# Reciprocal square roots by a GpSimd power throughout, and query projections filled up to 128 rows

## The chip, the cores and the metric

The kernel runs on one core of a Trainium2 chip. The metric is device time in microseconds (us) of one execution, from the first to the last instruction and what lies around it. The five engines are TensorE (PE in the profile, with its weight loads PEld), VectorE (DVE), ScalarE (ACT), GpSimd (POOL) and SyncE (SP, which issues the DMAs).

## The reference

Two transformer blocks follow one another on 512 tokens of 1024 features; the second also carries 256 context tokens. Everything is float32.

```python
def first_block(...):                      # once
    h = rmsnorm(x) * (1 + sc1) + sh1       # sc, sh, g: c_act @ w_ada
    q_a, k_a, v_a, q_d, k_d, v_d, z_d, b_d, a_d = split(h @ w_in)
    y_attn  = dilated_attention(q_a, k_a, v_a, rel_bias)      # 8 heads
    q, k, v = split(silu(causal_conv(concat(q_d, k_d, v_d))))
    q, k    = l2norm(q) * 64 ** -0.5, l2norm(k)               # per head
    o       = chunk_gated_delta_rule(q, k, v, g(a_d), sigmoid(b_d))
    y_delta = rmsnorm(o, norm_g) * silu(z_d)                  # per head
    x = x + g1 * (concat(y_attn, y_delta) @ w_out)
    x = x + g2 * swiglu(rmsnorm(x) ...)
def second_block(...):                     # two layers
    # half step of a gated FFN on h and on the context
    z  = modulate(rms_norm(h)) @ w_in      # 1376 columns
    q  = rms_norm(z[..., 256:448], g_q) @ w_uq       # 192 -> 4 heads x 96
    kv = rms_norm(z[..., 448:576], g_kv) @ w_ukv     # 128 -> 4 heads x 128
    # Fourier mixer, attention over h and context, gating unit
    # (its v is rms-normed per head), pooling mixer; then w_out
    # second half step; the context goes on only in layer 0
```

Every rmsnorm and l2norm takes one reciprocal square root per token, or per token and head.

## The kernel before, in words

Activations lie as 128 features by tokens. A weight comes in units of 128x1024: SP loads it (L183), ScalarE rounds it to a form that TensorE reads in one pass ("whi", L186), VectorE makes the rest ("wlo", L187), and a product takes three passes: whi by the high part of the activation, whi by its low part, wlo by its high part (`mm`, L128). Products of plain float32 operands are issued as one instruction each and take two passes in the trace. Transposes and broadcasts along features also go through TensorE (`tr`, L162).

The code is written as generators that a planner of the kernel interleaves. It counts the columns of every matmul (`mm` adds them to `self.clock`), and a generator's `yield 2.0` says after how many us of such work it wants to go on. The order of the instructions on each engine comes from the tile framework's scheduler, which weighs what each instruction costs and what it waits for; so a change of instructions on VectorE can move rows of the other engines too.

Reciprocal square roots come from one helper, `rsqrt` (L87). Up to two columns it is a scaling on VectorE (L97) and a power of -0.5 on GpSimd (L98). From three columns on it is eleven small VectorE instructions (L108 to L118): the scaling, a first guess from the bits, and two rounds of correction. Sixteen places have more than two columns: the first norm "n1" (128x4, L1470); in each of the four pairs of heads of the delta net one for q and k (128x16, `delta`, L728, tiles rsxd to rsyd) and one for the output (128x8, L895); in the second block the key and query norms of the latent tokens (128x4, `col_rsqrt`, L984, two in each layer) and the gating unit (128x16 twice, 128x8 once, L1283). All other norms have two columns.

In the first block, `delta_prep` (L667) makes the convolutions of q, k and v of a pair of heads (tiles "cv", L682), `delta_gates` (L614) makes decay and beta (gu, gs, gpoly, gx, then a matmul psg and gc), and `delta` (L688) goes on: GpSimd multiplies the decay matrices by masks (L717, L719), TensorE sums squares of q and k into psT, `rsqrt` follows, VectorE copies its result to rq (L730), ScalarE spreads it (L660), and TensorE transposes that to psb (L162), on which the rest of the pair stands. Attention tiles of other heads and weight products fill TensorE between.

In the second block `kvq` (L992) makes queries. The 192 normed features lie in two tiles, c0 (128 rows) and c1 (64 rows), and the weights in `wuq[0]` (128 rows) and `wuq[1]` (64 rows, `small_w`, L953). `pq(j)` (L1073) multiplies 128 columns of weights in two matmuls, the second of 64 rows:

```python
self.mm(ps[:, :T], self.wuq[0][:, j*P : (j+1)*P], c0[:, :T], True, False)
self.mm(ps[:, :T], self.wuq[1][0:64, j*P : (j+1)*P], c1[0:64, :T], False, True)
```

There are eleven such products: four for the latent tokens (T = 512) in each layer and three for the context (T = 256) in layer 0.

Of the kernel before, what the change touches and what calls it, by code (L numbers as in the profile page):

```python
# [9 lines left out]
F32 = mybir.dt.float32  # L10
F32R = mybir.dt.float32r
BF16 = mybir.dt.bfloat16
I32 = mybir.dt.int32
U8 = mybir.dt.uint8
AF = mybir.ActivationFunctionType
ALU = mybir.AluOpType
# [13 lines left out]
P = 128  # L30
# [3 lines left out]
EPS = 1e-6  # L34
# [47 lines left out]
class Kernel:  # L82
# [4 lines left out]
    def rsqrt(self, v, scale, shape, key):  # L87

        nc, sm = self.nc, self.small
        n = 1  # L90
        for d in shape[1:]:
            n *= d
        if n <= 2:
            x = sm.tile([P, n], F32, tag="rs_x", name=f"rsx{key}")
            y = sm.tile([P, n], F32, tag="rs_y", name=f"rsy{key}")
            xv = x.rearrange("p (a b) -> p a b", a=shape[1]) if len(shape) == 3 else x
            nc.vector.tensor_scalar(xv, v, float(scale), EPS, op0=ALU.mult, op1=ALU.add)  # L97
            nc.gpsimd.tensor_tensor(out=y, in0=x, in1=self.minus_half[:, 0:n], op=ALU.pow)  # L98
            return y
        x = sm.tile([P, n], F32, tag="rs_x", name=f"rsx{key}")  # L100
        y = sm.tile([P, n], F32, tag="rs_y", name=f"rsy{key}")
        a = sm.tile([P, n], F32, tag="rs_a", name=f"rsa{key}")
        b = sm.tile([P, n], F32, tag="rs_b", name=f"rsb{key}")
        xv = x
        if len(shape) == 3:
            xv = x.rearrange("p (a b) -> p a b", a=shape[1])
        V = nc.vector
        V.tensor_scalar(xv, v, float(scale), EPS, op0=ALU.mult, op1=ALU.add)  # L108
        V.tensor_scalar(y.bitcast(I32), x.bitcast(I32), -0.5, float(0x5F1FFFF9), op0=ALU.mult, op1=ALU.add)
        V.tensor_mul(a, y, y)  # L110
        V.tensor_mul(a, a, x)
        V.tensor_scalar(a, a, -0.703952253, 0.703952253 * 2.38924456, op0=ALU.mult, op1=ALU.add)
        V.tensor_mul(y, y, a)
        V.tensor_mul(a, y, y)
        V.tensor_mul(a, a, x)
        V.scalar_tensor_tensor(b, a, -10.0 / 3.0, a, op0=ALU.add, op1=ALU.mult)
        V.tensor_scalar(b, b, 0.375, 1.875, op0=ALU.mult, op1=ALU.add)
        V.tensor_mul(y, y, b)  # L118
        return y

    def ax1(self, name):
# [831 lines left out]
    def small_w(self, l, keep):  # L953

        nc, A, G = self.nc, self.A, self.G
        self.gcols = self.cp.tile([P, 8], F32, tag=f"gcols{l}", name=f"gcols{l}")
        nc.sync.dma_start(out=self.gcols, in_=A["gcols"][l])
        self.wukv = G.get("k" if keep else "t", "k")
        nc.sync.dma_start(out=self.wukv, in_=A["w_ukv"][l])
        self.wuq = [G.get("k" if keep else "t", "k"), G.get("k" if keep else "t", "k")]  # L960
        nc.sync.dma_start(out=self.wuq[0], in_=A["w_uq"][l, 0:128])
        nc.sync.dma_start(out=self.wuq[1][0:64, :], in_=A["w_uq"][l, 128:192])

    def zproj(self, s, u):


        halves = s.T == TL and any(x[2][0] is s for x in self.later)
        w = self.wunit(self.W2, u)
        ps = self.mm1("pz")
        for c0, c1 in ((0, 256), (256, 512)) if halves else ((0, s.T),):  # L970
            self.settle(s, c0, c1)
            for k in range(KD):
                ah, al = (x[:, c0:c1] for x in s.h[k][:2])
                wh, wl = w[0][:, k * P : (k + 1) * P], w[1][:, k * P : (k + 1) * P]
                self.mm(ps[:, c0:c1], wh, ah, k == 0, False)
                self.mm(ps[:, c0:c1], wh, al, False, False)
                self.mm(ps[:, c0:c1], wl, ah, False, k == KD - 1)
                if k == 3 or (c1 - c0 == TL and k in (1, 5)):
                    yield 1.3
            if c1 < s.T:  # L980
                yield 1.3
        return ps
# [9 lines left out]
    def kvq(self, s, l, rope, key, query):  # L992

        nc, V, G = self.nc, self.nc.vector, self.G
        T = s.T
        kh, vv = s.kv(l)
        s.vv = vv
        ps = yield from self.zproj(s, 0)
        held = []

        def pair():
            if T == TL:
                return G.get("t", "k"), G.get("t", "k")
            x = G.get("t", "k")
            held.append(x)
            return x[:, 0:T], x[:, T : 2 * T]
# [8 lines left out]
        ps = yield from self.zproj(s, 1)  # L1015
        if query:
            c1, sq1 = pair()
            nc.scalar.activation(sq1[0:64, :T], ps[0:64, :T], AF.Square)
            nc.scalar.activation(c1[0:64, :T], ps[0:64, :T], AF.Identity, scale=self.gcols[0:64, 2:3])
        if rope is not None:  # L1020
# [13 lines left out]
        if query:  # L1034
            ps = yield from self.zproj(s, 2)
# [13 lines left out]
        for j in range(2):  # L1049
            ps = self.ax1("pk")  # L1050
# [8 lines left out]
        for t in range(0, s.ntt, 2):  # L1059
            ps = self.ax1("pv")  # L1060
# [12 lines left out]
        def pq(j):  # L1073
            ps = self.ax1("pqh")
            self.mm(ps[:, :T], self.wuq[0][:, j * P : (j + 1) * P], c0[:, :T], True, False)
            self.mm(ps[:, :T], self.wuq[1][0:64, j * P : (j + 1) * P], c1[0:64, :T], False, True)
            return ps
        pr = pq(2)
        if rope is not None:
            t1, t2 = G.get("t", "k"), G.get("t", "k")  # L1080
            V.tensor_mul(t1, pr, rope[0])
            yield 1.7
            pr = pq(3)
            V.tensor_mul(t2, pr, rope[1])
            V.tensor_add(t1, t1, t2)
            yield 1.7
            for h in range(4):
                (nc.scalar.copy if h % 2 else V.tensor_copy)(qh[h][64:96, :], t1[32 * h : 32 * h + 32, :])
            G.put(t1, t2)
        else:  # L1090
            for h in range(4):
                (nc.scalar.copy if h % 2 else V.tensor_copy)(qh[h][64:96, :T], pr[32 * h : 32 * h + 32, :T])
            yield 0.9
        for j in range(2):
            ps = pq(j)
            for a in range(2):
                (nc.scalar.copy if a else V.tensor_copy)(qh[2 * j + a][0:64, :T], ps[64 * a : 64 * a + 64, :T])
            yield 1.7 * T / TL
# [320 lines left out]
    def build_(self, st, stop):  # L1419
        tc, nc, A = self.tc, self.nc, self.A  # L1420
# [21 lines left out]
        G = self.G  # L1442
        self.ones = self.cp.tile([P, 2], F32, tag="ones", name="ones")
        nc.vector.memset(self.ones, 1.0)
        self.minus_half = self.cp.tile([P, 8], F32, tag="mhalf", name="mhalf")
        nc.vector.memset(self.minus_half, -0.5)
        cv = self.load_cvec("cva", A["c"])
        mods = self.cp.tile([P, 48], F32, tag="mods1", name="mods1")
# [36 lines left out]
        for k in range(KD):  # L1485
# [9 lines left out]
            n = len(first)  # L1495
# [34 lines left out]
        v = []  # L1530
# [21 lines left out]
        for t in range(4):  # L1552
            f = collections.deque([attn] * MUL[t][0])
# [463 lines left out]
```

## Time and profile before

| what | us |
|---|---|
| time, median of 3 runs (lowest to highest) | 3309.32 (3308.56 to 3309.61) |
| profiled execution | 3308.47 |
| its span, first to last instruction | 3306.7 |
| PE busy | 3241.5 (98%) |
| DVE busy | 2036.8 (62%) |
| ACT busy | 1065.2 (32%) |
| POOL busy | 58.5 (2%) |

The span lies 1.8 us below the execution's own time. Busy time is counted from start to end of an instruction. In the timeline a row gives start, duration, engine, line, operation with out<-in, the number of instructions taken together, and in brackets the idle time of the engine ahead of it and what ended it. A 512-column pass follows the one before in some 0.21 to 0.23 us though the row of a single one reads 0.39, because the row runs from start to modelled end.

### The profile page before, as it was taken

The page shows a single profiled execution, that of the slowest core. Times are in us where ns is not written, and L with a number is a line of the kernel's source. Part 1 is how long each engine was busy: PE and PEld are TensorE (multiplying, and loading weights), DVE is VectorE, ACT ScalarE, POOL GpSimd, SP SyncE. Part 2 cuts the span into 40 slices and gives each one's busy share as a digit, 9 for nine tenths or more (in the row PEclk, how much of TensorE's full clock was granted, in tenths as well). Part 3 has the DMA queues.
Part 4 walks back from the last instruction along what each step waited for, and adds up shares of the span by engine and source line. Part 5 has one row for each costly group of instructions (what it writes and reads, how often), then busy time and mean ns, then how long its engine had stood idle before and what let it go on. Part 6 is the DMA issues. An engine that isn't in the chain of part 4 may idle for free.

```text
span 3306.7 us, 45936 instructions
## 1 busy us (share of the span) xinstructions
PE 3241.5 (98%) x18536; PEld 2705.1 (82%) x18536; DVE 2036.8 (62%) x3812; ACT 1065.2 (32%) x1782; POOL 58.5 (2%) x95
## 2 busy tenths in 40 slices
PE   6999999999999999999999999999999999999998
PEld 5778788888888888977888888888888888798887
DVE  7777785776856556667865454585554447673334
ACT  4444342224222222436522222242221235542222
POOL 0101000000000000000000000000000000000000
PEclk9999999999999999999999999999999999999999
DMA  8333254542433333222133232233332212233331
GB/s 268 103 111 95 81 158 153 161 145 78 159 97 106 103 107 100 83 87 90 58 120 96 83 101 85 88 101 110 112 106 83 89 52 79 60 109 96 96 96 58
DMA packets 105321, 344.12 MB, mean 104 GB/s; under 512 B 14402, under 2 KB 20459, under 8 KB 105108
## 3 DMA queue, kind: packets, MB, share of 16 engines
q1 hardware_dynamic: 105108, 341.17, 33.1%
q8 instruction: 146, 2.39, 0.3%
q14 instruction: 67, 0.55, 0.0%
HBM read 339.01 MB, written 4.74 MB: 104 GB/s over the span
## 4 chain that ended last, share of the span: by engine, by line
PE 93%; DVE 4%; issue 1%; ACT 1%; DMA 1%; POOL 0%; SPq 0%; POOLq 0%; DVEq 0%; ACTq 0%
PE psg L128 24%; PE psu L128 24%; PE psd L128 21%; PE psdc L128 6%; PE pz L128 4%; PE pp L128 3%; PE pss L128 2%; PE pso L128 2%; PE psv L128 2%; PE psY L128 1%; PE pst L162 1%; PE pqh L128 1%; DVE dump L246 0%; DVE wlo_w_in L187 0%; PE psb L162 0%
## 5 line engine op out<-in xcount | busy, mean ns | idle before, releaser
L186 ACT CAST whi_f<-wraw_f 128x1024 fp32r<-128x1024 f32 x264 | 276.5, 1050 | 716.6 <-PE psdc L128 238.1
L187 DVE TENSOR_TENSOR wlo_f<-wraw_f,whi_f 128x1024 fp32r<-128x1024 f32 x264 | 322.6, 1223 | 205.9 <-ACT whi_f L186 199.7
L128 PE MATMUL psu<-r,whi_f 128*128 128x512 f32 (+1 forms) x1504 | 446.1, 379 | 0.0
L128 PE MATMUL psg<-r,whi_f 128*128 128x512 f32 (+1 forms) x1504 | 443.8, 377 | 0.0
L128 PEld LDWEIGHTS psu<-r,whi_f 128*128 128x128 f32 x1504 | 277.1, 189 | 55.8
L128 PE MATMUL psd<-r,whi_f 128*128 128x512 f32 (+1 forms) x1152 | 321.8, 358 | 0.2 <-DVE xl L497 0.2
L128 PEld LDWEIGHTS psg<-r,whi_f 128*128 128x128 f32 x1504 | 273.2, 188 | 51.9
L408 DVE TENSOR_TENSOR sg<-sg,psu 128x512 f32<-128x512 f32 x110 | 75.5, 686 | 383.6 <-PE psu L128 382.3
L246 DVE CUSTOM_DVE_ANT_0 dump<-ada_w_ada,cva 128x1024 bf16<-128x1024 f32 x192 | 234.6, 1222 | 119.7 <-DMA ada_w_ada<-in_w_ada 118.8
L128 PE MATMUL psu<-r,wlo_f 128*128 128x512 f32 (+1 forms) x752 | 285.1, 379 | 0.0
L128 PE MATMUL psg<-r,wlo_f 128*128 128x512 f32 (+1 forms) x752 | 284.1, 378 | 0.0
L497 DVE SCALAR_TENSOR_TENSOR xl<-psd,ml,xl 128x512 f32<-128x512 f32 (+1 forms) x272 | 176.4, 654 | 152.4 <-PE psd L128 151.1
L128 PEld LDWEIGHTS psd<-r,whi_f 128*128 128x128 f32 x1152 | 184.4, 188 | 20.9 <-DVE xl L497 0.5
L128 PE MATMUL psu<-c,whi_f 128*128 128x512 f32 x528 | 189.5, 397 | 0.0
L128 PE MATMUL psg<-c,whi_f 128*128 128x512 f32 x528 | 188.3, 395 | 0.0
L128 PE MATMUL psd<-r,wlo_f 128*128 128x512 f32 (+1 forms) x528 | 187.3, 355 | 0.0
L128 PEld LDWEIGHTS psu<-r,wlo_f 128*128 128x128 f32 x752 | 141.8, 189 | 28.1
L128 PEld LDWEIGHTS psg<-r,wlo_f 128*128 128x128 f32 x752 | 141.6, 188 | 26.9
L497 DVE SCALAR_TENSOR_TENSOR xc<-psdc,mc,xc 128x256 f32<-128x256 f32 x320 | 150.6, 478 | 6.5 <-PE psdc L128 4.2
L128 PE MATMUL psdc<-r,whi_f 128*128 128x512 f32 x392 | 151.9, 393 | 0.0
L128 PE MATMUL psd<-y,whi_f 128*128 128x512 f32 (+1 forms) x512 | 150.9, 362 | 0.0
L128 PE MATMUL psu<-c,wlo_f 128*128 128x256 f32 x528 | 149.0, 282 | 0.0
(758 smaller groups left out, 6328.0 us busy)
## 6 DMA issues: line engine op xcount, KB each, us to landing
wraw_f<-in_f SPq DMA_DIRECT2D x264, 512.0 KB, 3.5
ada_w_ada<-in_w_ada SPq DMA_DIRECT2D x192, 512.0 KB, 3.6
wraw_ffn<-in_ffn SPq DMA_DIRECT2D x66, 512.0 KB, 3.6
wraw_w_in<-in_w_in SPq DMA_DIRECT2D x64, 512.0 KB, 3.5
wraw_w_out<-in_w_out SPq DMA_DIRECT2D x28, 512.0 KB, 3.5
bias<-bias SPq DMA_DIRECT2D x8, 320.0 KB, 5.7
xl<-in_x SPq DMA_DIRECT2D x8, 256.0 KB, 7.7
k<-bias SPq DMA_DIRECT2D x8, 256.0 KB, 3.6
```

What stands on the lines that cost most here:

```text
L128: self.nc.tensor.matmul(out, lhsT=lhsT, rhs=rhs, start=start, stop=stop)
L162: self.nc.tensor.transpose(out, in_, self.ident[:k, :k])
L186: nc.scalar.copy(hi, raw)
L187: nc.vector.tensor_sub(lo, raw, hi.bitcast(F32))
L246: job = nc.vector.tensor_tensor_reduce(out=dump, in0=raw, in1=cv, scale=1.0, scalar=0.0, op0=ALU.mult, op1=ALU.add, accum_out=dst[:, nb : ...
L408: nc.vector.tensor_mul(sg, sg, pu)
L497: nc.vector.scalar_tensor_tensor(x, q, gates[s][:, m : m + 1], x, op0=ALU.mult, op1=ALU.add)
```

## The change

Two edits. `rsqrt` loses its eleven-instruction form: all sixteen places above now do what the two-column places did, one VectorE scaling (now L96) and one GpSimd power (now L97); the tile of exponents grows from 8 to 16 columns. And the second tile of the query weights and of the normed query features get zeros in rows 64 to 127, written by GpSimd, so that both matmuls of `pq` read 128 rows.

```diff
@@ rsqrt
-        if n <= 2:
-            ...
-            return y
         x = sm.tile([P, n], F32, tag="rs_x", name=f"rsx{key}")
         y = sm.tile([P, n], F32, tag="rs_y", name=f"rsy{key}")
-        a = sm.tile([P, n], F32, tag="rs_a", name=f"rsa{key}")
-        b = sm.tile([P, n], F32, tag="rs_b", name=f"rsb{key}")
-        ...
-        V.tensor_scalar(xv, v, float(scale), EPS, op0=ALU.mult, op1=ALU.add)
-        V.tensor_scalar(y.bitcast(I32), x.bitcast(I32), -0.5, float(0x5F1FFFF9), op0=ALU.mult, op1=ALU.add)
-        V.tensor_mul(a, y, y)
-        V.tensor_mul(a, a, x)
-        ...
-        V.tensor_mul(y, y, b)
+        xv = x.rearrange("p (a b) -> p a b", a=shape[1]) if len(shape) == 3 else x
+        nc.vector.tensor_scalar(xv, v, float(scale), EPS, op0=ALU.mult, op1=ALU.add)
+        nc.gpsimd.tensor_tensor(out=y, in0=x, in1=self.minus_half[:, 0:n], op=ALU.pow)
         return y
@@ small_w
         nc.sync.dma_start(out=self.wuq[1][0:64, :], in_=A["w_uq"][l, 128:192])
+        nc.gpsimd.memset(self.wuq[1][64:128, :], 0.0)
@@ kvq
             c1, sq1 = pair()
+            nc.gpsimd.memset(c1[64:128, :T], 0.0)
@@ pq
-            self.mm(ps[:, :T], self.wuq[1][0:64, j * P : (j + 1) * P], c1[0:64, :T], False, True)
+            self.mm(ps[:, :T], self.wuq[1][:, j * P : (j + 1) * P], c1[:, :T], False, True)
@@ build
-        self.minus_half = self.cp.tile([P, 8], F32, tag="mhalf", name="mhalf")
+        self.minus_half = self.cp.tile([P, 16], F32, tag="mhalf", name="mhalf")
```

Line numbers after the helper fall by 21. On PE the order of the rows changes in the first block alone; from there on it stays. Three places show it.

On POOL at the first pair of heads, before: a copy and a clearing, then the six multiplications by masks (k is a slot of an arena, m_low and m_cum are masks), then clearings of tiles for the next step.

```order
L774 COPY k_19_141<-id_487 128x512
L801 MEMSET k_21_143 64x512
L717 ISA
L717 TENSOR_TENSOR k_6_128<-k_7_129,m_low 64x4x64 x2
L719 TENSOR_TENSOR k_7_129<-k_7_129,m_cum 128x512
L717 TENSOR_TENSOR k_6_128<-k_0_122,m_low 64x4x64 x2
L719 TENSOR_TENSOR k_0_122<-k_0_122,m_cum 128x512
L849 MEMSET k_16_138 128x512
L850 MEMSET k_17_139 128x512
```

On POOL at the same place, after:

```order
L753 COPY k_19_141<-id_476 128x512
L780 MEMSET k_21_143 64x512
L696 TENSOR_TENSOR k_6_128<-k_7_129,m_low 64x4x64 x2
L696 TENSOR_TENSOR k_6_128<-k_0_122,m_low 64x4x64
L698 TENSOR_TENSOR k_7_129<-k_7_129,m_cum 128x512
L696 TENSOR_TENSOR k_6_128<-k_0_122,m_low 64x4x64
L698 TENSOR_TENSOR k_0_122<-k_0_122,m_cum 128x512
L97 TENSOR_TENSOR rsyd_681<-rsxd_680,mhalf 128x16
L828 MEMSET k_16_138 128x512
```

A power (rsyd from rsxd, 16 columns) has come in behind the six multiplications and ahead of the clearings, and one multiplication by m_low now stands ahead of the first by m_cum.

On DVE at the first convolutions, before: wlo_w_in_8 is the low part of the eighth weight unit, cv a convolution step; gx, beta and gs belong to the gates.

```order
L187 TENSOR_TENSOR wlo_w_in_8_565<-wraw_w_in_8_562,whi_w_in_8_564 128x1024
L682 SCALAR_TENSOR_TENSOR cv<-pp,conv_w,cv 128x511
L631 TENSOR_TENSOR gx<-psT,dtb 128x32
L682 SCALAR_TENSOR_TENSOR cv<-pp,conv_w,cv 128x510
L633 TENSOR_SCALAR beta<-beta 128x32
L645 TENSOR_SCALAR gx<-gx 128x32
L682 SCALAR_TENSOR_TENSOR cv<-pp,conv_w,cv 128x509
L634 RECIPROCAL beta<-beta 128x32
L637 TENSOR_SCALAR gs<-gu 128x32
L682 SCALAR_TENSOR_TENSOR cv<-pp,conv_w,cv 128x511
L638 RECIPROCAL gs<-gs 128x32
```

On DVE around the same weight unit, after:

```order
L661 SCALAR_TENSOR_TENSOR cv<-pp,conv_w,cv 128x511
L613 RECIPROCAL beta<-beta 128x32
L616 TENSOR_SCALAR gs<-gu 128x32
L661 SCALAR_TENSOR_TENSOR cv<-pp,conv_w,cv 128x510
L617 RECIPROCAL gs<-gs 128x32
L661 SCALAR_TENSOR_TENSOR cv<-pp,conv_w,cv 128x509
L618 TENSOR_TENSOR gs<-gs,gu 128x32
L166 TENSOR_TENSOR wlo_w_in_8_554<-wraw_w_in_8_551,whi_w_in_8_553 128x1024
L619 TENSOR_TENSOR gs_495<-gs 128x32
L661 SCALAR_TENSOR_TENSOR cv<-pp,conv_w,cv 128x511
L620 TENSOR_SCALAR gpoly<-gs_495 128x32
L166 TENSOR_TENSOR wlo_w_in_1_610<-wraw_w_in_1_607,whi_w_in_1_609 128x1024
```

wlo_w_in_8 stood ahead of all nine convolution steps and now stands behind six of them (the last three of the six are in these rows); wlo_w_in_1 comes four rows on. On PE, a product with whi_w_in_1 has come between the second and the third pass of the product with unit 8.

On DVE at the end of the gates, before: gpoly and gx end in the input of the matmul psg, and gc is read from it.

```order
L187 TENSOR_TENSOR wlo_w_in_2_627<-wraw_w_in_2_624,whi_w_in_2_626 128x1024
L643 SCALAR_TENSOR_TENSOR gpoly<-gpoly,gs_506 128x32
L682 SCALAR_TENSOR_TENSOR cv<-pp,conv_w,cv 128x510
L643 SCALAR_TENSOR_TENSOR gpoly<-gpoly,gs_506 128x32
L682 SCALAR_TENSOR_TENSOR cv<-pp,conv_w,cv 128x509
L643 SCALAR_TENSOR_TENSOR gpoly<-gpoly,gs_506 128x32
L916 COPY k_8_130<-psv 128x256
L643 SCALAR_TENSOR_TENSOR gpoly<-gpoly,gs_506 128x32
L187 TENSOR_TENSOR wlo_w_in_11_771<-wraw_w_in_11_768,whi_w_in_11_770 128x1024
L643 SCALAR_TENSOR_TENSOR gpoly<-gpoly,gs_506 128x32 x3
L644 SCALAR_TENSOR_TENSOR gpoly<-gpoly,gs 128x32
L646 SCALAR_TENSOR_TENSOR gx<-gpoly,gx 128x32
```

On DVE at the end of the gates, after:

```order
L625 SCALAR_TENSOR_TENSOR gx<-gpoly,gx 128x32
L626 SCALAR_TENSOR_TENSOR gx<-gx,expa 128x32
L166 TENSOR_TENSOR wlo_w_in_2_616<-wraw_w_in_2_613,whi_w_in_2_615 128x1024
L630 COPY gc<-psg 128x32
L631 TENSOR_TENSOR kd<-psg,gc 128x32
L691 TENSOR_TENSOR k_7_129<-psG,gc 128x512
L691 TENSOR_TENSOR k_0_122<-psG,gc 128x512
L634 TENSOR_TENSOR bg<-beta,eg 128x32
L895 COPY k_8_130<-psv 128x256
L96 TENSOR_SCALAR rsxd_680<-psT 128x16
L166 TENSOR_TENSOR wlo_w_in_11_749<-wraw_w_in_11_746,whi_w_in_11_748 128x1024
L709 COPY rq<-rsyd_681 128x16
```

The gates now run through to gx and gc; wlo_w_in_2 and wlo_w_in_11, which stood between their steps, come later, wlo_w_in_11 directly ahead of the copy rq, which waits for the power on POOL.

## Rows read from the trace of the kernel before

**Rows 1.** The page: busy time by engine, and the chain that ended last.
```profile
PE 3241.5 (98%) x18536; PEld 2705.1 (82%) x18536; DVE 2036.8 (62%) x3812; ACT 1065.2 (32%) x1782; POOL 58.5 (2%) x95
PE 93%; DVE 4%; issue 1%; ACT 1%; DMA 1%; POOL 0%; SPq 0%; POOLq 0%; DVEq 0%; ACTq 0%
```

**Rows 2.** Stretches: busy us (instructions) by engine, granted clock, DMA share, GB/s.
```profile
20.00:40.00 20.00, 10.99 (x33) 6.54 (x34) 19.73 (x43) 5.81 (x7) 0.00 (x0) 1.00 0.78 267
2770.00:2790.00 20.00, 19.99 (x100) 12.88 (x99) 14.98 (x30) 10.82 (x22) 1.02 (x3) 1.00 0.25 80
```

**Rows 3.** Waits of PE: what for, us in total, times, longest.
```profile
PE psb L162 <- ACT k L660: 5.5, 3, 2.8
PE pst L162 <- DVE st L576: 2.3, 1, 2.3
PE psbn L162 <- DVE rsyn L118: 2.3, 1, 2.3
PE psg L128 <- DVE gx L647: 1.1, 1, 1.1
```

**Rows 4.** Timeline of a latent query projection: start, us, engine, operation [idle before].
```profile
2777.51 0.30 PEld L128 LDWEIGHTS pqh<-t,t 128*128 128x128 f32 x2 [0.76 <-DVE wlo_w_in L187]
2778.56 0.29 PEld L128 LDWEIGHTS pqh<-k,t 64*128 64x128 f32 x2 [0.76 <-issue]
2779.62 0.19 PEld L128 LDWEIGHTS pz<-r,whi_w_in 128*128 128x128 f32 x1 [0.76 <-issue]
```

**Rows 5.** Timeline, context query projection.
```profile
1486.56 1.03 PE L128 MATMUL pv<-k,k 128*128 128x256 f32 x4
1487.21 0.41 PEld L128 LDWEIGHTS pqh<-k,k 128*128 128x128 f32 x2
1487.43 1.22 PE L128 MATMUL pqh<-k,k 128*128 128x256 f32 x4
1488.58 0.39 PE L128 MATMUL pz<-r,whi_w_in 128*128 128x256 f32 x1
```

**Rows 6.** Timeline, first norm.
```profile
19.74 0.16 DVE L108 TENSOR_SCALAR rsxn<-pss 128x4 f32<-128x4 f32 x1 [1.75 <-PE pss L128]
24.12 0.74 DVE L1491 SCALAR_TENSOR_TENSOR k<-xl,gs_attn,psbn 128x512 f32<-128x512 f32 x1
```

**Rows 7.** GpSimd's power: ns min/median/max, starts, forms.
```profile
L98 POOL TENSOR_TENSOR rsyf<-rsxf,mhalf x2: 692/1154/1616, 795.0 to 813.2; 128x2 f32<-128x2 f32 x2
```

**Rows 8.** One of the eleven VectorE steps, 16 columns wide, as in Rows 7.
```profile
L113 DVE TENSOR_TENSOR rsyd<-rsyd,rsad x4: 176/932/1294, 81.4 to 327.7; 128x16 f32<-128x16 f32 x4
```

**Rows 9.** Timeline, first pair of heads of the delta net.
```profile
75.97 0.18 DVE L108 TENSOR_SCALAR rsxd<-psT 128x16 f32<-128x16 f32 x1 [0.26 <-PE psT L128]
81.03 1.28 POOL L719 TENSOR_TENSOR k<-k,m_cum 128x512 f32<-128x512 f32 x1
83.42 0.17 DVE L730 COPY rq<-rsyd 128x16 f32<-128x16 f32 x1
84.82 1.42 PE L162 MATMUL psb<-ident,k 128*128 128x128 f32 x11 [1.99 <-ACT k L660]
```

**Rows 10.** Timeline, VectorE: eighth weight unit, a convolution step, another unit, the gates' end.
```profile
56.46 1.22 DVE L187 TENSOR_TENSOR wlo_w_in<-wraw_w_in,whi_w_in 128x1024 fp32r<-128x1024 f32 x1 [2.58 <-ACT whi_w_in L186]
57.61 0.74 DVE L682 SCALAR_TENSOR_TENSOR cv<-pp,conv_w,cv 128x511 f32<-128x511 f32 x1
69.68 1.23 DVE L187 TENSOR_TENSOR wlo_w_in<-wraw_w_in,whi_w_in 128x1024 fp32r<-128x1024 f32 x1 [1.17 <-ACT whi_w_in L186]
71.94 0.19 DVE L647 SCALAR_TENSOR_TENSOR gx<-gx,expa 128x32 f32<-128x32 f32 x1
```

**Rows 11.** Stretch at the eighth unit, tile pp alone, as in Rows 2.
```profile
58.00:63.00 5.00, 5.00 (x22) 4.12 (x23) 3.23 (x5) 0.75 (x2) 1.00 0.94 338
```

**Rows 12.** Timeline, second pair of heads.
```profile
151.62 0.17 DVE L108 TENSOR_SCALAR rsxd<-psT 128x16 f32<-128x16 f32 x1
160.56 0.17 DVE L730 COPY rq<-rsyd 128x16 f32<-128x16 f32 x1
```

More of the change, by code (lines that the diff above doesn't have):

```diff
@@ L92, in rsqrt @@
             n *= d
-        if n <= 2:
[L94 to L98, printed above, removed]
-            return y
         x = sm.tile([P, n], F32, tag="rs_x", name=f"rsx{key}")
         y = sm.tile([P, n], F32, tag="rs_y", name=f"rsy{key}")
-        a = sm.tile([P, n], F32, tag="rs_a", name=f"rsa{key}")
-        b = sm.tile([P, n], F32, tag="rs_b", name=f"rsb{key}")
[L104 to L107, printed above, removed]
-        V.tensor_scalar(xv, v, float(scale), EPS, op0=ALU.mult, op1=ALU.add)
-        V.tensor_scalar(y.bitcast(I32), x.bitcast(I32), -0.5, float(0x5F1FFFF9), op0=ALU.mult, op1=ALU.add)
-        V.tensor_mul(a, y, y)
-        V.tensor_mul(a, a, x)
[L112 to L117, printed above, removed]
-        V.tensor_mul(y, y, b)
+        xv = x.rearrange("p (a b) -> p a b", a=shape[1]) if len(shape) == 3 else x
+        nc.vector.tensor_scalar(xv, v, float(scale), EPS, op0=ALU.mult, op1=ALU.add)
+        nc.gpsimd.tensor_tensor(out=y, in0=x, in1=self.minus_half[:, 0:n], op=ALU.pow)
         return y
```

## The prediction

> **What bounds the kernel now.** I read the page first: PE is busy for 3241.5 of 3306.7 us, and 93% of the chain that ended last is PE [rows 1]. So an edit counts only where PE waits, or where it shortens or lengthens PE's own work; 2036.8 us of VectorE count for nothing by themselves. Stretches of time come next: from 20 to 40 us PE is busy for 10.99 us and VectorE for 19.73, so the start belongs to VectorE, while at the second layer's queries PE is busy 19.99 of 20 us [rows 2]. Last, the waits of PE name what the change could touch: psb 5.5 us in three waits (the spread of rq), pst 2.3, psbn 2.3 (the first norm's result), psg 1.1 [rows 3]. Together that is 11.2 us, all that a shorter square root could give back on PE, 0.34% of the time.
>
> **Query projections, -3.9.** Both halves of a latent product come in two passes of 512 columns. From load to load they take 1.05 and 1.06 us, each with a gap of 0.76 us ahead of the load, at full clock [rows 4, 2]. What the passes take without a change of height is seen at the context: four 256-column passes of pv, of 128 rows throughout, go from 1486.56 to 1487.43, 0.87 us; the four of pqh, with a change down to 64 rows and one back, go from 1487.43 to 1488.58, 1.15 us [rows 5]. So a context product would save 0.28. A latent one has twice the columns: 1.05 + 1.06 - 2 x 0.87 = 0.37. Eight latent and three context products give 8 x 0.37 + 3 x 0.28 = 3.8; I take 3.9, between this and the 4.5 that 22 changes at 0.2 would give. PE has no idle time there, so it comes off the end whole. The zeros are written by POOL, 2% busy [rows 1], long before they are read. Bounds: 0 (the gap belongs to something else than the height) to -4.5.
>
> The gap has a rival reading. The 128-row load of pqh at 1487.21 starts while the pv passes from 1486.56 (1.03 us) still run [rows 5]; the loads at which the height changes wait 0.76 [rows 4]. The Trainium skill (TensorE: Matmul & The Clock Gate, The mechanism) says that a load overlaps running matmuls only when it goes to other row groups of the array. By that rule loads of full height could not be laid beside full-height passes, and the filling-up would gain nothing, for a sum 3.9 us higher; this row speaks against it.
>
> **What a wide power costs.** The trace has GpSimd's power at two columns only: 0.692 us, and 1.616 at its longest [rows 7]. Were the 0.692 all fixed, 4, 8 and 16 columns would cost 0.7 too; were all of it per column, 1.4, 2.8 and 5.5. No row shows which. The ends are far apart and no row is nearer to one; I take their geometric means: 1.0, 1.4 and 2.0 us.
>
> Why it was long once: VectorE ran a subtraction with two inputs in SBUF at the same time, and the other way round a 16-column VectorE step takes 0.176 us at best and 1.294 while POOL multiplies [rows 8]. The Trainium skill (SBUF — State Buffer, Who interferes with whom) says that GpSimd and such VectorE instructions lock each other out of a shared port for a whole instruction. If each of the delta net's eight new powers lost the 0.92 us between the shortest and the longest row in this way, the sum would be up to 7.4 us higher. By that rule the trace agrees; but the lockout also hits the ten steps that go away, so it is a rival below and no term.
>
> **First norm.** VectorE is the bound. Ten steps go, about 2 us (PE's psbn waits 2.3 for them [rows 3]); in their place VectorE stands still from rsxn at 19.74 through the power (1.0), four transposes (about 1.1) until k, which was at 24.12 and can now run near 22.3 [rows 6]. But the low part of the weights and a modulation product, 2.4 us, that stood between, are only pushed behind it. Net about -0.6. At 0.7 for the power it is -0.9, at 1.4 it is -0.2.
>
> **First pair of heads, +3, the start included.** This is where the new order bites. The eighth unit's low part, at 56.46, moves behind six convolution steps of 0.74: 6 x 0.74 = 4.4, to an end near 62.0 instead of 57.7 [rows 10]. PE stands at that unit at about 57.9 and now waits, some 4 us, less the start's 0.6. Against this the gates end earlier: gx at 71.94 stood behind another low part at 69.68 that had waited 1.17 for ScalarE, 1.2 us of its own, and behind one more [rows 10]; 2 to 4.5 us of that go, and with them PE's 1.1 for gx [rows 3]. POOL's last mask multiplication ended at 82.31 [rows 9] and would end near 79; the power stands queued behind it, so rq comes at about 79 + 2.0 + 0.2 = 81.2 instead of 83.42 and psb at 82.6 instead of 84.82. That sounds like a gain of 2.2, but by the order of the rows PE has less work before psb than before: 18 passes of 512 columns and 9 of 256 have moved behind it, at 22 passes in 5 us [rows 11], 0.23 each and half of that for the narrow ones, 18 x 0.23 + 9 x 0.12 = 5.2 us. What is moved must still be done, so the pair costs 5.2 - 2.2 = +3. The start's gain is inside this, for its 0.6 moved everything in it. VectorE waits for the power in rq, with the multiplications for v and the next low part queued behind it; PE's filling work hides that, as long as it lasts. Bounds: 0 (gates 4.5 earlier, power 0.7) to +7 (gates 2 earlier, power 5.5).
>
> **The other pairs and the output norms, -1.5.** The second pair's square root goes from rsxd at 151.62 to rq at 160.56, 8.9 us, because the steps alternate with others and with POOL's multiplications [rows 12]. With one power it can come some 5 us sooner; PE, though, waits there only for pst (2.3), and for psb 0.7 and 2.8 in the third and fourth pair, 5.8 in all [rows 3]. By the order of the rows PE has less filling work between psT and psb there too, which takes part of it back, and VectorE stands still for each power. I take -1.5, with -6 (all the waits go) and +9 (three powers of 5.5 and four of 2.8 uncovered) as ends. The column norms and the gating unit of the second block lie where PE has work beside them [rows 2]: 0.
>
> **Sum.** -3.9 + 3.0 - 1.5 = -2.4. The profiled execution took 3308.47, so 3306.1; the median of the runs was 0.85 higher, so 3306.9. A difference under 0.2%, 6.6 us, is about what a measurement of this kernel can't tell from none.
>
> **Rivals.**
> - *The powers are cheap and the waits go.* All powers at 0.7, the pst and psb waits of the later pairs gone (-6), the first pair at +1, the queries -4.5: -9.5, 3299.8. For it: two columns cost 0.692 and POOL is 2% busy; against: PE's filling work is also moved away. Chance 0.22.
> - *The powers cost per column.* At 5.5 and 2.8 us the first pair is +6.5, the later pairs and output norms +9, the queries -3.9: +11.6, 3320.9. VectorE waits in order for rq, and each pair's psb after it. The result gets slower than before from about 2.6 us for 16 columns, and measurably so from about 4. For it: a power of two columns costs 0.692, a VectorE step of 16 columns 0.176 [rows 7, 8]; against: a GpSimd multiplication of 512 columns takes 1.28 [rows 9]. Chance 0.11.
> - *Filling up gains nothing*: the gap of 0.76 belongs to these loads, whatever their height. -2.4 + 3.9, 3310.8. Against it the row of 1487.21 above. Chance 0.09.
> - *VectorE holds up the powers*, 0.92 us at each of the delta net's eight [rows 7]: -2.4 + 7.4, 3314.3. Against it: VectorE mostly stands at rq while the power runs. Chance 0.06.
> - The forecast, 3306.9, with 3302 to 3312 for itself: chance 0.52.
>
> The range reaches 3299 to 3317. Faster by over 0.2% (under 3302.7): nearly all of the first rival and a little of the forecast, 0.26; slower (over 3315.9): most of the second and a little of the last, 0.11; the rest, 0.63, the same.
>
> **What would show it.** Right: no gap ahead of pqh's loads, 1.7 instead of 2.1 us for a latent product; k of the first norm near 22.3; a PE wait of 3 to 4 us for wlo_w_in_8 near 58 us; no wait for gx; powers of 16 columns near 2 us, and rq of the second pair within 5 us of rsxd. Wrong: a 16-column power under 1 us or over 4; PE waits for psb of over 3 us in a later pair; or psT and the squares ahead of it so late that the earlier gates bring nothing.

## The result: 0.6% slower

| | before | after |
|---|---|---|
| median of 3 runs, us | 3309.32 (3308.56 to 3309.61) | 3328.58 (3328.23 to 3331.06) |
| profiled execution, its span, us | 3308.47, 3306.7 | 3331.06, 3329.0 |
| mean granted TensorE clock | 0.998 | 0.992 |

The ratio is 1.006, with a 95% interval from 1.0046 to 1.0073: slower, by 19.3 us in the medians, and outside the range of the forecast (3299 to 3317). The profiled execution is the slowest of its three, 2.5 us above the median, so what follows accounts for the 22.3 us between the two spans. The whole loss lies ahead of the first block's FFN. Its first gate product starts at 430.8 us before and at 455.2 after, 24.4 us later; from there to the end it is 2875.9 against 2873.8 us.

Stretches of the profile after: first that part as a whole, then the eight in which TensorE was granted half its clock (columns as in [rows 2]; 0.50 is 1.2 of 2.4 GHz).

```profile
0.00:455.20 455.20, 402.94 (x3591) 321.11 (x3591) 318.72 (x704) 180.52 (x317) 55.73 (x58) 0.95 0.40 127
34.59:37.99 3.40, 3.21 (x8) 2.54 (x9) 3.40 (x7) 0.70 (x1) 0.00 (x0) 0.50 0.72 231
61.89:68.71 6.82, 5.18 (x12) 4.12 (x13) 6.55 (x19) 4.07 (x7) 0.00 (x0) 0.50 0.87 305
85.79:92.60 6.81, 5.16 (x18) 4.61 (x19) 5.69 (x14) 1.14 (x2) 1.27 (x3) 0.50 0.24 77
167.71:177.94 10.23, 8.55 (x54) 6.31 (x53) 8.04 (x16) 2.25 (x7) 4.31 (x4) 0.50 0.17 51
256.45:263.27 6.82, 6.37 (x17) 4.68 (x18) 6.50 (x11) 3.62 (x6) 2.65 (x4) 0.50 0.11 18
348.61:352.02 3.41, 2.90 (x13) 2.90 (x14) 3.33 (x5) 1.41 (x2) 2.23 (x3) 0.50 0.00 0
427.12:430.52 3.40, 3.40 (x9) 2.52 (x10) 1.68 (x6) 1.59 (x4) 0.95 (x1) 0.50 0.00 0
437.36:440.76 3.40, 3.40 (x21) 2.67 (x20) 0.00 (x0) 0.57 (x2) 0.00 (x0) 0.50 0.81 236
```

And the kernel before, up to the same instruction, with its two stretches:

```profile
0.00:430.80 430.80, 386.09 (x3591) 307.35 (x3591) 331.36 (x792) 179.74 (x316) 35.69 (x49) 0.99 0.42 134
162.27:165.67 3.40, 3.40 (x17) 2.98 (x17) 2.52 (x5) 2.14 (x4) 0.52 (x1) 0.50 0.00 0
332.94:336.34 3.40, 3.40 (x15) 2.84 (x13) 2.27 (x5) 0.56 (x1) 0.52 (x1) 0.50 0.00 0
```

From these rows comes the account of the 24.4 us. PE's idle time is length less busy: 44.7 before, 52.3 after, +7.6. Busy time at half clock is 6.8 before and 38.2 after (the eight rows added). Half of it is counted as lost, since 512-column passes follow one another in 0.43 us there (64.12 to 64.97 for two) and in 0.23 at the full clock: 3.4 and 19.1, +15.7. The remaining +1.1 are longer passes. In this execution two thirds of the loss are TensorE's clock; in the trace of the changed kernel's second measurement, with the FFN at 454.4, the three terms are 7.4, 13.0 and 3.2.

What fell where, in the waits of PE after (columns as in [rows 3]):

```profile
PE psb L141 <- ACT k L639: 9.9, 4, 4.2
PE pst L141 <- DVE sc L556: 4.5, 4, 2.3
PE pp L107 <- DVE wlo_w_in L166: 3.3, 2, 2.8
...
PE pv L107 <- DVE t L1040: 2.4, 1, 2.4
...
PE psbn L141 <- POOL rsyn L97: 2.0, 2, 1.3
```

The waits for psb have grown from 5.5 to 9.9 us, the one for wlo_w_in_8 is new, and so is pv, in the second block. The first pair of heads, to be held against [rows 9], in the timeline:

```profile
81.85 1.29 POOL L698 TENSOR_TENSOR k<-k,m_cum 128x512 f32<-128x512 f32 x1
...
83.10 2.90 POOL L97 TENSOR_TENSOR rsyd<-rsxd,mhalf 128x16 f32<-128x16 f32 x1
86.04 0.17 DVE L709 COPY rq<-rsyd 128x16 f32<-128x16 f32 x1 [4.87 <-POOL rsyd L97]
...
87.44 0.90 PE L141 MATMUL psb<-ident,k 128*128 128x128 f32 x3 [4.25 <-ACT k L639]
```

The power stands behind the masks, takes 2.90 us, and VectorE waits 4.87 us for it and PE 4.25.

### The profile page after: what moved, and what is told of

The parts are those of the page before. It is cut to its first block, busy times and chain, and to the rows that moved or that the text cites. A ratio compares the mean times of both kernels' runs of the same rounds, so it can differ in the third digit from the quotient of the medians.

```text
span 3329.0 us, 45821 instructions
## 1 busy us (share of the span) xinstructions
PE 3253.4 (98%) x18536; PEld 2719.9 (82%) x18536; DVE 2012.8 (60%) x3652; ACT 1066.8 (32%) x1782; POOL 94.4 (3%) x116
## 4 chain that ended last, share of the span: by engine, by line
PE 53%; DVE 2%; ACT 1%; DMA 1%; issue 0%; POOL 0%; POOLq 0%; DVEq 0%; ACTq 0%
PE psg L107 14%; PE psu L107 14%; PE psd L107 13%; PE psdc L107 4%; PE pz L107 3%; PE pss L107 1%; PE pso L107 1%; PE pst L141 1%; PE psv L107 1%; PE pqh L107 0%; DMA wraw_f<-in_f 0%; DMA ada_w_ada<-in_w_ada 0%; DVE dump L225 0%; DVE wlo_f L166 0%; PE pv L107 0%
```

## The experiments

Times are medians; each kernel was timed beside the one before on the same chip (which took 3309.0 to 3310.4 us there).

| kernel | us | ratio to before, 95% interval |
|---|---|---|
| filling up alone | 3306.16 | 0.9989 [0.9980, 0.9998] |
| power alone, everywhere | 3336.78 | 1.0082 [1.0069, 1.0096] |
| filling up, power in the second block only | 3309.36 | 1.0001 [0.9992, 1.0010] |
| changed, wide powers replaced by multiplications | 3311.36 | 1.0004 [0.9995, 1.0013] |
| changed, again | 3332.24 | 1.0070 [1.0053, 1.0087] |
| changed, two waits filled | 3330.18 | 1.0066 [1.0051, 1.0081] |
| changed, more work asked for beside the power | 3334.04 | 1.0077 [1.0062, 1.0092] |
| power in the first norm only | 3312.56 | 1.0010 [1.0001, 1.0019] |
| power in the 16-column roots only | 3310.65 | 1.0004 [0.9994, 1.0013] |
| power in the 8-column roots only | 3314.93 | 1.0021 [1.0012, 1.0030] |
| power in 16- and 8-column roots | 3320.57 | 1.0036 [1.0023, 1.0049] |
| power in first norm and 16-column roots | 3320.68 | 1.0037 [1.0023, 1.0052] |
| first norm only, again | 3313.23 | 1.0007 [0.9998, 1.0015] |
| first norm only, wait at unit 8 filled | 3309.39 | 1.0000 [0.9991, 1.0008] |
| changed, three waits filled | 3328.47 | 1.0052 [1.0037, 1.0068] |

**Filling up alone.** The kernel before with the second edit of the change (small_w, kvq and pq of its diff) and nothing else.

> The filling-up with zeros alone, square roots as before. PE's order of instructions is that of before. Theory (it works as forecast, the loss is all in the square roots): 3.6 to 3.9 us less than before, about 3305.5, no gap of 0.76 us ahead of the loads of pqh, a latent product in 1.7 us instead of 2.1. Rival (the zeros written by GpSimd or the fuller passes cost something elsewhere, and the second block gained by something else): within 1 us of before.

It is 2.8 us faster, a little less than expected: in its trace the FFN starts 1.4 us later than before, with one more stretch at the lower clock, 85.7 to 89.1 us. The loads of the last latent product show the reason (timeline, as in [rows 4]): no gap of 0.76 but 0.24, and 0.86 us from half to half where it was 1.05.

```profile
2779.00 1.02 PE L128 MATMUL pqh<-t,t 128*128 128x512 f32 x2
...
2779.43 0.19 PEld L128 LDWEIGHTS pqh<-k,t 128*128 128x128 f32 x1 [0.24 <-issue]
...
2779.86 1.02 PE L128 MATMUL pqh<-k,t 128*128 128x512 f32 x2
2779.86 0.19 PEld L128 LDWEIGHTS pqh<-k,t 128*128 128x128 f32 x1 [0.24 <-issue]
```

Between the same instructions of PE on either side, the queries take 1.55 us less in the first layer, 0.74 at the context and 1.58 in the second layer: 3.9, as forecast.

**Power alone, and power in the second block only.** The first is the change without those lines; the second restricts the power to the names of the second block:

```diff
-        if n <= 2:
+        if n <= 2 or key[0] in "lg":
```

> The power in all square roots, query projections as before. Theory (all of the loss is here, 23.5 us of it in the first block's profile): some 22 to 25 us slower than before, 3331 to 3334. Rival (the two edits disturb each other): under 15 us slower.

> Eleven steps again in the first block (first norm, delta net); the power in the second block's wide square roots, and the filling-up. PE's order is that of before. Theory (the loss is all in the first block; in the second, VectorE waits 3 us for the 16-column power of the gating unit and PE 2.4 us behind it): filling up gives 3.7, the power takes 2 to 2.5 back, so 1.0 to 2 us faster than before, about 3308. Rival (the power costs nothing there): 3.7 us faster, 3305.5, as with the filling-up alone.

The power alone costs 27.8 us, a little more than expected. In the second block it costs 3.2 (3309.36 against 3306.16), where 2 to 2.5 were expected: all that filling up had brought. The trace of that kernel shows where:

```profile
1414.30 2.90 POOL L98 TENSOR_TENSOR rsygl<-rsxgl,mhalf 128x16 f32<-128x16 f32 x1 [6.19 <-DVE rsxgl L97]
...
1417.24 0.69 DVE L1288 TENSOR_TENSOR t<-t,rsygl 128x512 f32<-128x512 f32 x1 [3.01 <-POOL rsygl L98]
1417.85 0.68 DVE L1059 TENSOR_TENSOR t<-t,psbl0q 128x512 f32<-128x512 f32 x1
...
1419.26 1.10 PE L128 MATMUL pv<-k,t 128*128 128x256 f32 x4 [2.37 <-DVE t L1060]
```

The gating unit's multiplication waits 3.01 us for the 16-column power, and the queries' own, which had everything it needed, stands behind it on VectorE; PE waits 2.37.

**The power's duration or the order.** The changed kernel, wide powers as multiplications (these norms are left out):

```diff
-in1=self.minus_half[:, 0:n], op=ALU.pow)
+in1=(self.minus_half if n <= 2 else self.thousandth)[:, 0:n], op=ALU.pow if n <= 2 else ALU.mult)
```

> The changed kernel with each power of more than two columns replaced by a GpSimd multiplication of the same tiles by 0.001 (so these norms are left out); every engine keeps its order of instructions, only the duration falls, from 1.0, 1.6 and 2.9 us to some 0.2. Theory 1 (the new order of the rows leaves PE with too little work beside its waits, whatever the power takes): still 10 us or more slower than before, wait for wlo_w_in_8 unchanged at 2.8, TensorE at its lower clock near 62 to 69 us and in at least three later stretches. Theory 2 (the powers' own duration makes the waits): within 5 us of before, psb waits under 2 us, at most three stretches at the lower clock.

Neither theory alone holds. The first lines are the wide powers of the changed kernel (columns as in [rows 7]), the second the multiplications in their place, the third their kernel up to the FFN:

```profile
L97 POOL TENSOR_TENSOR rsyd<-rsxd,mhalf x4: 2895/2901/2905, 83.1 to 344.6; 128x16 f32<-128x16 f32 x4
...
L97 POOL TENSOR_TENSOR rsyd0o<-rsxd0o,mhalf x1: 1638/1638/1638, 153.1 to 153.1; 128x8 f32<-128x8 f32 x1
```
```profile
L97 POOL TENSOR_TENSOR rsyd<-rsxd,thousandth x4: 217/221/223, 81.3 to 329.3; 128x16 f32<-128x16 f32 x4
```
```profile
0.00:438.90 438.90, 397.58 (x3591) 317.16 (x3591) 318.42 (x705) 180.52 (x317) 38.75 (x58) 0.97 0.41 132
```

In the same order, with 0.22 us for 2.90, the FFN starts at 438.9 instead of 455.2: in these two executions 16.3 of the 24.4 us hang on the powers' duration, 8.1 on the new order. Of those 8.1, idle time is -3.4 (438.9 - 397.6 = 41.3, less than the 44.7 before); what is lost is the lower clock, 26.6 us busy at it, half of 19.8 more than before, and 1.7 in longer passes. PE idles less than before and is slower. The profiled execution, 3313.45 us, was 2.1 above this kernel's median. By the medians the order costs less, 2.4 us over the kernel before, or some 5 with the 2.8 of filling up taken out. Theory 2 had the time and the waits for psb (1.6 at most); theory 1 had the wait for wlo_w_in_8 (2.8) and the stretches at the lower clock, six up to the FFN.

**Which powers.** Five kernels are the one before with the power at some places alone; the condition of the first and of the third:

```diff
-        if n <= 2:
+        if n <= 2 or key in ("d0", "d1", "d2", "d3"):
...
+        if n <= 2 or key in ("d0o", "d1o", "d2o", "d3o"):
```

> The kernel before with the power in the four 16-column square roots of the delta net alone; the rest, the first norm and the query projections as before. Theory (the 16-column powers make most of the loss): 8 to 16 us slower than before. Rival (the start's new order, with its wait for wlo_w_in_8, makes most of it): within 5 us of before.

> The kernel before with the power in the first norm alone (4 columns, 1.0 us in the changed kernel). By the rows this alone moves wlo_w_in_8 behind six convolution steps. Theory 1 (the start's new order makes most of the loss): PE waits 1.3 us for whi_w_in_1 and 2.8 for wlo_w_in_8, TensorE at its lower clock there, 8 to 15 us slower than before. Theory 2 (the output norms, or the powers of the delta net together, make it): within 5 us of before although the two waits are there.

> The kernel before with the power in the four 8-column square roots of the delta net's outputs alone (1.64 us each in the changed kernel). Theory 1 (the start makes most of the loss): within 3 us of before. Theory 2 (the output norms, or the powers of the delta net together): 5 to 12 us slower, waits of PE for psb or pst over 2 us in two pairs or more, and more stretches at the lower clock.

> The kernel before with the power in all eight square roots of the delta net, 16 and 8 columns. Theory 1 (the start): the sum of the two parts, within 5 us of before. Theory 2 (each pair now has too little PE work beside both powers): 10 to 18 us slower, although the 16-column ones alone cost 1.3.

> The kernel before with the power in the first norm and in the four 16-column square roots. Theory 1 (the start): 10 to 16 us slower, about as the first norm alone. Theory 2 (output norms or delta net as a whole): under 7 us slower. A third case, that only the start's order and the first pair together make the 4.25 us wait for psb: slower by 3 to 6 us more than the sum of the two single changes.

No one place makes the loss. Over the 3309.4 of before, the first norm adds 3.2, the 16-column roots 1.3 and the 8-column ones 5.6; in pairs 11.2 and 11.3, 4.3 and 6.8 more than their sums; all three come to some 24.6 (27.8 for the power alone, less the second block's 3.2). For the theory that the 16-column ones make most of it this is a miss, and so it is for the one that names the start's new order, although the waits at unit 8 are there with the first norm alone.

What grows in pairs is the waits: PE's idle time up to the FFN is 43.5, 43.2 and 43.9 us in the three single kernels, no more than the 44.7 before, and 48.9 and 48.8 in the pairs. The first pair's wait for psb is 2.16 with the first norm alone, 1.19 with the 16-column roots alone, 4.24 with both, as in the changed kernel: the third case of the last expectation, with more than its 3 to 6 us. This fits that each takes PE work from beside the other.

The 8-column roots took the time that theory 2 gave them, but not through its waits: 4.0 of their 4.9 us (to the FFN, in the profile) are PE passes that last longer at the full clock. Changes between 64-row and 128-row products explain little of that: the trace has 144 against 142, at the 0.18 us of a latent product's change an estimate of 0.4. The rest stays open.

**More work beside the power.** One number:

```diff
-        yield 3.0
+        yield 5.0
         ps = self.head_bcast(h3(br), "psb")
```

> The changed kernel with one number altered: the generator of a pair of heads asks for 5 us of other work between the wide square root and psb in place of 3, so the rows put more PE work beside the power (estimated from the rows at full clock 6.4, 10.9, 9.2 and 3.6 us in the four pairs, 3.6, 4.0, 7.2 and 5.0 in the changed kernel, 6.7, 10.2, 9.7 and 7.3 in the one before). Theory (power of 2.9 us with too little work beside it): PE's waits for psb in the first two pairs fall under 1.5 us, fewer stretches at the lower clock, 6 to 14 us faster than the changed kernel. Rival (it is the power's hold on VectorE and POOL, not the work beside it): within 4 us of the changed kernel.

A miss. The waits of the first two pairs for psb fall to 1.5 and 0, but pst (3.1), a product behind VectorE (2.9), the fourth pair's psb (3.7) and the last output norm's (2.7) wait instead. In its trace the FFN starts at 449.4 us, against 454.4 in the changed kernel's second trace, but from there to the end it takes 2881.1 us against 2876.7; why stays open.

**Filling waits.** Useless matmuls into the tile that the next instructions overwrite, in `head_bcast` for psb (first lines, five in the first pair and three in the fourth) and in `proj_g` for unit 8.

```diff
+        for _ in range(busy):
+            self.nc.tensor.matmul(ps, lhsT=self.ident, rhs=x, start=True, stop=True)
...
+        for _ in range(4 if u == 8 else 0):
+            self.nc.tensor.matmul(ps, lhsT=self.ident, rhs=s.X[:, 0, :], start=True, stop=True)
```

> The changed kernel once more, to stand beside the next three on the same chip: some 19 us slower than before, with TensorE at its lower clock in eight stretches of the first block, near 86 to 93 us and 349 to 352 us among them.

> The changed kernel with useless work added: five plain 512-column matmuls (ten passes, 4.3 us at the full clock) directly ahead of the first pair's psb, where PE waits 4.25 us, and three (2.6 us) ahead of the fourth pair's, where it waits 2.6. PE's other instructions keep their order; the results are not touched. Theory (a wait costs twice, once itself and once in the lower clock that follows it): the two stretches at the lower clock near 86 to 93 and 349 to 352 us go, and the kernel gets 3 to 5 us faster than the changed one although it does more work. Rival (the lower clock is no consequence of these waits): the stretches stay, time the same as the changed kernel or up to 3 us longer.

> The power in the first norm alone once more, as the one to compare with on the same chip: 3 us slower than before, TensorE at its lower clock for two stretches, near 34 to 41 and 61 to 68 us, more than before.

> The power in the first norm alone, with four useless plain 512-column matmuls (eight passes, 3.4 us at the full clock) ahead of the product with unit 8, where PE waits 1.3 and 2.8 us; nothing else moves in PE's order, the results are not touched. Theory (the waits bring the lower clock): the stretch from 61 to 68 us goes, the first block is 3 us shorter, and the kernel as fast as before or 1 us slower although it does 3.4 us more work on PE. Rival (the lower clock comes from something else): the stretch stays, time the same or up to 3.4 us longer.

> The changed kernel with three waits filled by useless work: unit 8 (four matmuls), psb of the first pair (five) and of the fourth (three), 10.2 us of work in all. Theory: the stretches near 62 to 69 and 86 to 93 us go, 5 to 9 us faster than the changed kernel. Rival: the same or up to 10 us slower than the changed kernel.

With the first norm alone (the trace of its first measurement), the stretch behind the wait at unit 8, and under it that wait:

```profile
0.00:435.20 435.20, 391.71 (x3590) 313.06 (x3590) 329.92 (x782) 179.86 (x316) 38.20 (x50) 0.97 0.42 133
...
61.25:68.08 6.83, 4.71 (x11) 3.74 (x12) 6.65 (x19) 4.10 (x8) 0.00 (x0) 0.51 0.92 323
```
```profile
60.14 0.39 PE L128 MATMUL psv<-whi_w_in,r 128*128 128x256 f32 x1 [1.28 <-ACT whi_w_in L186]
...
63.38 0.80 PE L128 MATMUL pp<-r,wlo_w_in 128*128 128x512 f32 x1 [2.84 <-DVE wlo_w_in L187]
```

And with the wait filled, the stretch and the filling:

```profile
0.00:432.30 432.30, 390.56 (x3599) 310.69 (x3599) 329.93 (x782) 179.90 (x316) 38.14 (x50) 0.99 0.42 134
58.00:65.00 7.00, 5.88 (x21) 3.33 (x22) 6.96 (x18) 6.50 (x12) 0.52 (x1) 1.00 0.82 303
```
```profile
58.28 3.70 PE L924 MATMUL pp<-xl,ident 128*128 128x512 f32 x8
...
63.69 0.50 PE L128 MATMUL pp<-r,wlo_w_in 128*128 128x512 f32 x1 [1.12 <-DVE wlo_w_in L187]
```

The lower clock at unit 8 is gone, and the kernel that does 3.7 us more on PE has a median 3.8 us lower (3313.23 to 3309.39; the intervals overlap). Of the eleven executions without the filling two, at a mean clock of 0.998, took 3308.6 and 3308.7, and eight at 0.996 a median of 3313.6: the same rows, told apart by the clock alone. The trace of the one of 3308.7 has the same 2.84 us of wait at unit 8 with 3.4 us at half clock behind it instead of 6.8. None follows its later waits of 2.2, 2.4 and 2.8 us; behind the same three waits the trace shown above has a stretch each.

In the changed kernel filling the first pair's wait took away the stretch near 87 to 94 us; the fourth pair's only moved, to 353.6. The gain is 2 us, about half of what was expected, and the executions overlap (3327.8 to 3333.0 against 3331.0 to 3333.3). With unit 8 filled too, both early stretches read 1.00:

```profile
0.00:450.80 450.80, 406.04 (x3614) 318.95 (x3614) 318.69 (x704) 180.00 (x317) 55.71 (x58) 0.98 0.40 128
61.90:68.70 6.80, 5.80 (x24) 4.21 (x23) 6.70 (x17) 4.32 (x8) 0.00 (x0) 1.00 0.80 286
85.80:92.60 6.80, 6.80 (x74) 5.51 (x74) 5.69 (x12) 0.28 (x1) 1.52 (x3) 1.00 0.25 77
```

Idle time is back at 44.8, as before the change. With 10.2 us of useless work the kernel stands 18.1 us above the one before; the changed kernel stood 19.3 and 22.9 us above it in its two measurements. No run shows a price for the added work, but the 5 to 9 us that were expected are not shown either.

What shows the cause is the rows of the clock. The two waits at unit 8 are there in nine of the traces, and a stretch at half clock lies at or behind them in all nine; it is missing in both traces in which they are filled. The first pair's wait of 4.2 us is there in four, with a stretch in all four, and filled in two, with none. So these waits do bring the clock down; waits of 2 to 2.8 us did in some executions and not in others. The Trainium skill (TensorE: Matmul & The Clock Gate, HAM oscillation — how this bites in real kernels) says that waits between groups of matmuls, there for DMAs, put TensorE back to its lower clock, so that the work behind them starts slow. The traces agree, but not for every wait: each of the first six stretches after, and both of before, begins in a wait of PE or less than 2 us behind one, while the 1.99 us for psb at 84.82 before [rows 9] have none behind them.

## Why the prediction was wrong

The mechanism was largely there; the sum left out what a wait brings with it.

- **The step that failed is the sum's price of a wait.** "PE stands at that unit at about 57.9 and now waits, some 4 us" was right (1.3 for the product put in between, 2.8 for the low part), as was "no wait for gx". But every wait was counted at its own length, and TensorE's clock at 1.00 throughout, although the trace of before has two stretches at 0.50 behind waits for pst and psb, 162 and 333 us. That is 15.7 of the 24.4 us (13.0 of 23.7 in the second trace); idle time came out 6.1 us over the forecast.
- **First pair, +3.** psb came at 87.44 instead of 82.6: POOL's last mask multiplication ended at 83.1, not near 79, and the power took 0.9 us more. That is 2.6 later than before, and with the forecast's 5.2 us of work moved behind it +7.8. Of this 4.2 are the lower clock (half of the 3.2 and 5.2 us busy in the first two stretches), so +3.6 without it.
- **Later pairs and output norms, -1.5.** Idle time rose by 7.6 up to the FFN, where the first pair's +3 and this -1.5 made +1.5. The pairs' roots did get quicker, as said: rq of the second pair 3.6 us behind rsxd where it took 8.9 [rows 12]. But the rows had less PE work beside them, and the output norms, which the prediction gave no term of their own, cost 5.6 us alone, the dearest of the three.
- **Second block, 0.** It was 3.2 by the medians (1.1 and 2.7 in the traces, from the FFN to the end, against filling up alone): VectorE's order put a multiplication that was ready behind one that waited for the power.
- **The power.** 1.01, 1.64 and 2.90 us at 4, 8 and 16 columns, for 1.0, 1.4 and 2.0. The rival "the powers cost per column" had the sign and, with the first block's 16.3 us, the larger part of the cause, though at 2.9 instead of 5.5; its point from which the change is measurably slower, 4 us, was too high for want of the clock: between the forecast's 2.0 us and that rival's 5.5 lie 14 us, so by this line 2.9 us would give +1.2. Its +9 for the later pairs does not come out of its own terms: three powers of 5.5 and four of 2.8 are 27.7. VectorE held up none of the delta net's powers, as the last rival had it: its four of 16 columns took 2.895 to 2.905 us.
- **Queries, -3.9.** Right to 0.1 in the trace, though 22 changes at 0.2 are 4.4 and not 4.5.
- **First norm.** k of the first norm at 22.23, forecast 22.3; its gain went into the wait at unit 8, as said.

The rule that would have let filling up gain nothing (the Trainium skill, TensorE: Matmul & The Clock Gate, The mechanism) is not borne out here: with full height throughout, the load at 2779.43 lies beside passes that run from 2779.00.

## What to carry to other kernels

An engine that is busy 98% of the time at the full clock has two prices for a wait: the wait, and slower work after it; before making a chain shorter, look in the granted clock's rows for what the waits already cost, and ask how much work the new order leaves beside each of them. What it costs to move small work to a slow engine is set by what stands in order behind the reader of the result, not by what the other engine saves: here 24 us less on VectorE went with 19 us more in all. Of the two edits, filling up alone is the version to keep, 0.1% faster than before; the power belongs where its reader has nothing ready behind it.

## What the runs showed of the hardware

- The lower clock also came without a wait. Ahead of the stretch at 427 us after, PE shows no idle time, but six us of mostly small products, many of 64 columns or 2 (timeline). The kernel before has the same rows in the same order (second lines), and the clock behind them stays at 1.00:

```profile
420.47 2.92 PE L107 MATMUL pso<-k,k 128*128 128x64 f32 x32
...
424.54 1.05 PE L107 MATMUL psT<-sel,k 128*128 128x2 f32 x8
...
426.95 0.67 PE L107 MATMUL psd<-r,whi_w_out 128*128 128x512 f32 x1
```
```profile
400.09 2.92 PE L128 MATMUL pso<-k,k 128*128 128x64 f32 x32
...
404.16 1.05 PE L128 MATMUL psT<-sel,k 128*128 128x2 f32 x8
...
406.57 0.50 PE L128 MATMUL psd<-r,whi_w_out 128*128 128x512 f32 x1
```

  Of the seventeen traces five show the lower clock there, among them one of the two of the changed kernel. So these rows alone don't bring it, and no run took this apart.
- GpSimd's power costs by its columns: 0.70, 1.01, 1.64, 2.90 us for 2, 4, 8, 16, that is 0.38 + 0.157 a column; a multiplication of 16 columns took 0.22 in its place.
- Executions of one and the same kernel differ by the granted clock: those of before took 3308.4 us in the median at a mean clock of 0.998 (40 of them) and 3310.5 at 0.997 (38); the kernel with multiplications went from 3306.5 at 0.997 to 3316.3 at 0.993.
